# Two attentions of a transformer kernel: a zero-padded tile that stays allocated, and a second buffer for copies out of PSUM

## The chip, the cores and the metric

The kernel runs on one core of a Trainium2 chip. The metric is the device time of one execution in microseconds, the median of several runs. Five engines work side by side, each on its own queue of instructions in a fixed order: PE (matmuls; its weight loads are shown as PEld), DVE, ACT, POOL, and SP, which issues the DMAs. An instruction at the head of a queue that has to wait holds up everything behind it on that engine.

## The reference, cut to what matters

Two layers over 1024 tokens of width 1024. Layer 0 mixes with a hybrid attention (8 dilated heads and 4 pairs of differential heads), layer 1 with a latent attention of 16 heads; after each comes a feed-forward block with a short convolution. Both attentions are causal softmax attentions over blocks of 128 queries:

```python
def one_block(args):
    i, qi = args
    qpos = i * Q_BLOCK + jnp.arange(Q_BLOCK)
    causal = kpos[None, :] <= qpos[:, None]
    s = jnp.einsum('bqhd,bkhd->bhqk', qi, k).astype(jnp.float32) * scale
    p = jax.nn.softmax(jnp.where(causal, s, -jnp.inf), axis=-1)
    return jnp.einsum('bhqk,bkhd->bqhd', p.astype(v.dtype), v)
```

The kernel carries each fp32 operand as a high and a low part and adds several products of the parts.

## The kernel before, in words

Work runs through these stages in turn: the first attention with its projections (to about 540 us), the first feed-forward block, the second attention (about 1318 to 1664 us), the second feed-forward block.

In both attentions a head is worked off in two groups, g = 0 (query blocks 0 to 3, in the order 1, 0, 3, 2) and g = 1 (blocks 4 to 7). For each block `scores` has PE form the scores in a `wide` PSUM tile (L250, two such tiles), DVE take scale, mask and row maximum into `prob` (L259), and ACT the exponential (L262). `turn_parts` then writes the normalised probabilities as two fp16 parts into `hl`: the high part by ACT (L286) and the low part by DVE (L287), except for block 3 (`LP`), where ACT scales (L283) and POOL makes both parts (L121 and L110). SP transposes `hl` by DMA into `pTa`, `pTb` or `pT` (L290, L293), and `weigh` has PE multiply these with the values V (L327).

Blocks 0 and 1 share one tile, `hl01` (shown in the trace as `hl`): four quarter tiles for key blocks and query blocks, of which the quarter "key block 1, query block 0" must be zero. Before, each group g = 0 allocates this tile anew from one buffer, and POOL writes its zeros (L277) before the parts go in. The new tile's first write has to wait until the DMA transposition (L293) of the group before has read the old one. There are 28 such groups: 12 in the first attention, 16 in the second.

In the second attention, `prep(p)` makes queries, keys and values of the next pair of heads in the background, in a budget of PE time beside the current groups. `nope` multiplies into a PSUM tile `bank_t` (three of them serve all such work), ACT copies it to an SBUF tile `stage` (L1380), and POOL makes from it the high parts (L1384) and the low parts (L110) for two heads: four instructions for each copy. `values` does the same with `vs` (L1398), which shares the tag and so the buffer of `stage`: two POOL instructions for each copy (L121, L110). With one buffer, a copy waits until POOL is done with the one before. The first pair (p = 0) splits straight out of PSUM and uses no such copy.

The order of instructions on each engine is written when the program is built: the Tile layer plays the instructions against modelled durations (`schedule_with_timeline_sim=True`) and gives each engine the most urgent instruction whose inputs and buffers are ready in that model. Urgency is program order, with a bonus of 30 places for the maximum and the exponential. On the chip the order is fixed; when an instruction takes longer than the model had it, what stands behind it waits.

Of the kernel before, what the change touches and what calls it, by code (L numbers as in the profile page):

```python
# [11 lines left out]
F32 = mybir.dt.float32  # L12
F32R = mybir.dt.float32r
I32 = mybir.dt.int32
F16 = mybir.dt.float16
# [6 lines left out]
P = 128  # L22
# [24 lines left out]
def model_kernel(ctx: ExitStack, tc: tile.TileContext, a: dict, out: bass.AP, dbg: dict):  # L47
    nc = tc.nc
# [21 lines left out]
    def bank_p():  # L70
        if ps_lat[0]:
            return ps[0].tile([P, 512], F32, name="bank_p", tag="bank_p", bufs=1)
        return bank_t()
# [38 lines left out]
    def dma(out_, in_):  # L112
        out_, in_ = (v.bitcast(F32) if v.dtype == F32R else v for v in (out_, in_))
        nc.sync.dma_start(out=out_, in_=in_)

    def split(hi, lo, x, lo_eng=None):
        nc.scalar.copy(out=hi, in_=x)  # L117
        sub(lo_eng or nc.vector, lo, x, hi)

    def pool_split(hi, lo, x):  # L120
        nc.gpsimd.tensor_scalar(out=hi, in0=x, scalar1=1.0, scalar2=1.0, op0=ALU.mult, op1=ALU.mult)  # L121
        sub(nc.gpsimd, lo, x, hi)

    def mm3(out_, sh, sl, mh, ml, start, stop):
        nc.tensor.matmul(out_, sh, mh, start=start, stop=False)  # L125
        nc.tensor.matmul(out_, sh, ml, start=False, stop=False)  # L126
        nc.tensor.matmul(out_, sl, mh, start=False, stop=stop)  # L127
# [137 lines left out]
    def turn_parts(pt, l, top, i, pool, pts):  # L265

        r = pool.tile([P, 1], F32, name="rl", tag="rl", bufs=6)
        nc.vector.reciprocal(out=r, in_=l)
        nc.vector.tensor_scalar(out=r, in0=r, scalar1=top, scalar2=1.0, op0=ALU.mult, op1=ALU.mult)
        pair = MERGE and i < 2  # L270
        if not pair:
            hl = pool.tile([P, i + 1, 2, P], F16, name="hl", tag="hl", bufs=PH[1])
            hi, lo = hl[:, :, 0, :], hl[:, :, 1, :]
        else:
            if len(pts) == 2:
                hl = pool.tile([P, 2, 2, 2, P], F16, name="hl01", tag="hl01", bufs=1)
                nc.gpsimd.memset(hl[:, 1, :, 0, :], 0.0)  # L277
                pts.append(hl)
            hl = pts[2]
            hi, lo = hl[:, :i + 1, 0, i, :], hl[:, :i + 1, 1, i, :]  # L280
        v = pt.rearrange("p (k c) -> p k c", c=P)
        if i in LP:
            nc.scalar.activation(out=v, in_=v, func=AF.Copy, scale=r)  # L283
            pool_split(hi, lo, v)
        else:
            nc.scalar.activation(out=hi, in_=v, func=AF.Copy, scale=r)  # L286
            nc.vector.scalar_tensor_tensor(out=lo, in0=v, scalar=r, in1=hi, op0=ALU.mult, op1=ALU.subtract)  # L287
        if not pair:
            j = (i - 2) % 4 if MERGE and i < 4 else i % 4
            nc.sync.dma_start_transpose(out=pts[-1 if i > 3 else 1][:, :2 * (i + 1), j * P:(j + 1) * P],  # L290
                                        in_=hl.rearrange("p k s c -> p (k s c)"))
        elif len(pts) == 4:
            nc.sync.dma_start_transpose(out=pts[0].rearrange("p n (i q) -> p (n i) q", i=2),  # L293
                                        in_=hl.rearrange("p k s i c -> p (k s i c)"))
        else:
            pts.append(None)

    def new_pts(pool, g):
        if g:
            return [pool.tile([P, 16, 512], F16, name="pT", tag="pT", bufs=1)]  # L300
        return [pool.tile([P, 4, 256], F16, name="pTa", tag="pTa", bufs=1),
                pool.tile([P, 8, 256], F16, name="pTb", tag="pTb", bufs=1)]
# [489 lines left out]
    def open_pool(name, side="left"):  # L792
        return tc.alloc_tile_pool(name=name, bufs=1, side=side, reuse_waits="tile")
# [331 lines left out]
    pool = open_pool("hyb_n")  # L1125
# [20 lines left out]
        nc.sync.dma_start(out=d, in_=t)  # L1146
    pool.release()
    pool = open_pool("hyb_at", "right")
    made = []

    def tail_hyb():
# [168 lines left out]
    def new_QK(pool):  # L1320
        i = len(QK)
        QK.append([{n: pool.tile([P, 2, S], F32R, name=f"{n}{par}{i}") for n in "qk"}
                   for par in range(2)])
        for n in "qk":
            nc.gpsimd.memset(QK[i][1][n][0:32].bitcast(F32), 0.0)
# [13 lines left out]
    def prep(p):  # L1339

        qd = p // 2
        T = QK[p % 2]
        ws = slice((p % 2) * P, (p % 2 + 1) * P)
        if p % 2 == 0:
            quads[qd] = [kp.tile([P, 2, S], F32R, name="rhl", tag="rhl", bufs=1),
                         kp.tile([P, NB, 2, 2, P], F16, name="V4", tag="V4", bufs=2)]
        rhl, V = quads[qd]

        def turn(hf):
            pt = bank_p()  # L1350
            for j in range(4):
                nc.tensor.transpose(pt[:, j * P:(j + 1) * P],
                                    qr[:, hf * 4 + j, qd * P:(qd + 1) * P], ident)
            ts = slice(hf * 512, (hf + 1) * 512)
            split(rhl[:, 0, ts], rhl[:, 1, ts], pt)
            yield 428

        def q_rope(ts):
            for par in range(2):
                hd = (p % 2) * 2 + par  # L1360
                src = slice(hd * 32, hd * 32 + 32)
                dma(T[par]["q"][ROWS[par][1], :, ts], rhl[src, :, ts])

        def nope(hf):
            ts = slice(hf * 512, (hf + 1) * 512)
            for n, chunks in (("q", (0, 1)), ("k", (2,))):
                wh, wl = w[n]
                o = bank_p()
                for ci, c in enumerate(chunks):
                    mm3(o, wh[:, ci, ws], wl[:, ci, ws], cTh[:, c, ts], cTl[:, c, ts],  # L1370
                        ci == 0, ci == len(chunks) - 1)
                    if ci < len(chunks) - 1:
                        yield 640
                if p == 0:
                    for par in range(2):
                        rows = ROWS[par][0]
                        split(T[par][n][rows, 0, ts], T[par][n][rows, 1, ts], o[rows])
                else:
                    st = ap.tile([P, 512], F32, name="stage", tag="stage", bufs=1)
                    nc.scalar.copy(out=st, in_=o)  # L1380
                    for par in range(2):
                        rows = ROWS[par][0]
                        t = T[par][n][rows]
                        nc.gpsimd.tensor_scalar(out=t[:, 0, ts], in0=st[rows],  # L1384
                                                scalar1=1.0, scalar2=1.0, op0=ALU.mult, op1=ALU.mult)
                        sub(nc.gpsimd, t[:, 1, ts], st[rows], t[:, 0, ts])
                yield 640

        def values(hf):
            for b in range(4 * hf, 4 * hf + 4):  # L1390
                bs = slice(b * P, (b + 1) * P)
                o = bank_p()
                mm3(o[:, :256], cTh[:, 2, bs], cTl[:, 2, bs], w["v"][0][:, 0], w["v"][1][:, 0],
                    True, True)
                ov = o[:, :256].rearrange("p (h d) -> p h d", d=P)
                if p:
                    vs = ap.tile([P, 2, P], F32, name="vs", tag="stage", bufs=1)
                    nc.scalar.copy(out=vs, in_=ov)  # L1398
                    pool_split(V[:, b, :, 0], V[:, b, :, 1], vs)
                else:  # L1400
                    split(V[:, b, :, 0], V[:, b, :, 1], ov)
                yield 320

        halves = [slice(0, 512), slice(512, S)]
        if p == 0:
            w = qw[0]
            for hf in range(2):
                yield from turn(hf)
                q_rope(halves[hf])
                k_rope(0, halves[hf])  # L1410
                yield from nope(hf)
                yield from values(hf)
            return
        if p % 2 == 0:
            for hf in range(2):
                yield from turn(hf)
            next(quad_gen[-1])
        w = qw[qd]
        q_rope(slice(0, S))
        for hf in range(2):  # L1420
            yield from nope(hf)
        if p % 2 == 0:
            for hf in range(2):
                yield from values(hf)
        elif p < 7:
            quad_gen.append(quad_weights(qd + 1, bank_p))
            next(quad_gen[-1])
# [45 lines left out]
    PH[:] = BUF_MLA  # L1473
    psum("ps_mla")
    ap = open_pool("mla_at")
    new_QK(ap)
    k_rope(1, slice(0, S))
    run_slot([[groups[0][0](), groups[0][1], 0.0], [bgs[0], P_COST / 2 + V_COST / 2, 0.0]], None)
# [144 lines left out]
```

## Time and profile before

| | us |
|---|---|
| median of 3 runs | 2417.92 (2417.5 to 2418.85) |
| the profiled execution's own time | 2414.22 |
| its span from first to last instruction | 2412.4 |
| mean granted TensorE clock in the span | 0.979 of full speed |

Times in the rows are microseconds from the first instruction of the profiled execution. An engine's busy time in a stretch does not add up with that of the others, since they run side by side.

### The profile page before, as it was taken

What the parts mean: (1) busy time and instruction counts of PE and PEld (TensorE: products, weight loads), DVE (VectorE), ACT (ScalarE), POOL (GpSimd) and SP (SyncE); (2) the same over time, 40 slices, a digit from 0 to 9 for tenths busy, and PEclk for the clock granted to TensorE, in tenths of its full rate; (3) what the DMA queues carried; (4) which work ended last, traced back from release to release, by engine and by line L of the source; (5) the groups of instructions that cost most, each with busy time, mean ns of one, the idle gap of its engine ahead of it and who ended that gap; (6) DMA issues with size and microseconds to landing.
All of it is one profiled execution on the core that took longest, in us unless ns stands there. A gap on an engine that the chain in (4) does not pass through costs nothing. (4 is left out here: it accounts for less than half of the span.)

```text
span 2412.4 us, 32458 instructions
## 1 busy us (share of the span) xinstructions
PE 2222.4 (92%) x11216; PEld 1254.7 (52%) x11216; DVE 1941.0 (80%) x3265; ACT 1551.8 (64%) x2633; POOL 1115.2 (46%) x1157
## 2 busy tenths in 40 slices
PE   7999999898999999999999888889899999999998
PEld 5555566675444444343457666667644444434443
DVE  6777788848788888888786886875778888888887
ACT  6787776636766565666445887764576757575743
POOL 3233333116446464645126777741554656464621
PEclk9999999999999999999999998999999999999999
DMA  4566642651211111111031898797221112121101
GB/s 147 112 133 133 139 94 63 172 176 36 79 53 62 44 62 44 62 53 59 13 128 34 161 170 170 151 278 201 74 70 58 66 37 70 43 70 44 62 27 70
DMA packets 322358, 224.28 MB, mean 93 GB/s; under 512 B 279120, under 2 KB 282192, under 8 KB 321744
## 3 DMA queue, kind: packets, MB, share of 16 engines
q1 hardware_dynamic: 322192, 222.20, 35.5%
q8 instruction: 88, 1.44, 0.2%
q14 instruction: 78, 0.64, 0.1%
HBM read 123.59 MB, written 25.43 MB: 62 GB/s over the span
## 5 line engine op out<-in xcount | busy, mean ns | idle before, releaser
L572 PEld LDWEIGHTS <-up_h 128*128 128x128 f16 x2464 | 239.1, 98 | 319.2 <-issue 46.2
L262 ACT ACTIVATE prob<-prob,m 128x512 f32<-128x512 f32 (+7 forms) x256 | 197.5, 772 | 76.6 <-DVE m L259 61.1
L287 DVE SCALAR_TENSOR_TENSOR hl<-prob,rl,hl 128x896 f16<-128x896 f32 (+6 forms) x196 | 185.8, 957 | 41.3 <-ACT hl L286 40.0
L572 PEld LDWEIGHTS <-up_l 128*128 128x128 f16 x1232 | 120.8, 98 | 150.0 <-issue 7.9
L651 DVE SCALAR_TENSOR_TENSOR up_l<-up_raw,wsc,up_h 128x1024 f16<-128x1024 f32 x84 | 137.4, 1637 | 61.7 <-ACT up_h L650 61.7
L286 ACT ACTIVATE hl<-prob,rl 128x896 f16<-128x896 f32 (+6 forms) x196 | 149.0, 775 | 47.4 <-DVE prob L1031 15.1
L125 PE MATMUL bank_t<-hw_h,hTh 128*128 128x384 f16 x512 | 170.0, 334 | 7.4 <-ACT hw_h L650 4.4
L126 PE MATMUL bank_t<-hw_l,hTh 128*128 128x384 f16 x512 | 169.9, 333 | 0.6 <-DVE hw_l L651 0.5
L127 PE MATMUL bank_t<-hw_h,hTl 128*128 128x384 f16 x512 | 169.9, 332 | 0.0
L259 DVE CUSTOM_DVE_ANT_0 prob<-wide,maskc 128x256 f32<-128x256 f32 (+3 forms) x192 | 142.7, 750 | 23.5 <-PE wide L250 20.0
L731 PEld LDWEIGHTS <-qah 128*128 128x128 f16 x896 | 86.3, 98 | 124.0 <-issue 20.5
L250 PE MATMUL wide<-k,q 96*128 96x512 f32 (+7 forms) x576 | 131.7, 366 | 17.6 <-DVE m L259 17.2
L327 PEld LDWEIGHTS <-V 128*128 128x128 f16 x1064 | 97.0, 99 | 90.5 <-issue 33.7
L737 DVE SCALAR_TENSOR_TENSOR x<-bank_a,gun,x 128x512 f32<-128x512 f32 x168 | 124.4, 743 | 18.5 <-PE bank_a L731 14.9
L737 DVE SCALAR_TENSOR_TENSOR x<-bank_b,gun,x 128x512 f32<-128x512 f32 x152 | 112.7, 743 | 24.2 <-PE bank_b L731 24.2
L488 ACT ACTIVATE up_s<-up_raw 128x1024 f32<-128x1024 f32 x88 | 92.9, 1056 | 61.0 <-DVE up_l L651 33.4
L327 PE MATMUL bank_o<-pT,V 128*128 128x512 f16 (+3 forms) x608 | 120.3, 351 | 12.7 <-DMA pT<-hl 8.5
L110 POOL TENSOR_TENSOR up_l<-up_raw,up_h 128x512 f16<-128x512 f32 (+1 forms) x48 | 69.6, 1450 | 129.0 <-ACT up_h L117 75.0
L250 PEld LDWEIGHTS wide<-k,q 128*128 128x128 f32 (+1 forms) x576 | 98.7, 198 | 37.0 <-DVE m L259 22.9
L578 ACT COPY u<-prod 128x512 f32<-128x512 f32 x176 | 96.9, 572 | 29.2 <-PE prod L572 27.5
L650 ACT ACTIVATE dn_h<-dn_raw,dsc 128x1024 f16<-128x1024 f32 (+1 forms) x60 | 60.5, 1030 | 74.9 <-PE bank_b L731 52.3
L650 ACT ACTIVATE up_h<-up_raw,wsc 128x1024 f16<-128x1024 f32 x84 | 95.1, 1141 | 19.4 <-DVE wsc L459 14.6
(441 smaller groups left out, 7077.9 us busy)
## 6 DMA issues: line engine op xcount, KB each, us to landing
up_raw<-in_w_up_dram SPq DMA_DIRECT2D x88, 512.0 KB, 3.8
dn_raw<-in_ffn_w_down_dram SPq DMA_DIRECT2D x44, 512.0 KB, 3.2
hw_raw<-in_w_hyb_dram SPq DMA_DIRECT2D x32, 384.0 KB, 3.7
OTa<-ohl SPq DMA_DIRECT2D x16, 512.0 KB, 2.7
oa<-OTa SPq DMA_DIRECT2D x16, 512.0 KB, 6.3
OTb<-ohl SPq DMA_DIRECT2D x16, 512.0 KB, 3.4
x<-in_x_dram SPq DMA_DIRECT2D x8, 512.0 KB, 8.3
wo_raw<-in_hyb_w_out_dram SPq DMA_DIRECT2D x16, 256.0 KB, 3.3
```

Of the source, the lines that this page charges most:

```text
L125: nc.tensor.matmul(out_, sh, mh, start=start, stop=False)
L126: nc.tensor.matmul(out_, sh, ml, start=False, stop=False)
L127: nc.tensor.matmul(out_, sl, mh, start=False, stop=stop)
L250: nc.tensor.matmul(sp[:, h * 512:h * 512 + w], q[:, qs], k[:, c:c + w], start=n == 0, stop=n == len(passes) - 1)
L259: nc.vector.tensor_tensor_reduce(out=pv, in0=sv, in1=mv, scale=-scale, scalar=3e38, op0=ALU.add, op1=ALU.min, accum_out=m)
L262: nc.scalar.activation(out=pv, in_=pv, func=AF.Exp, bias=m, scale=-1.0, accum_out=l)
L286: nc.scalar.activation(out=hi, in_=v, func=AF.Copy, scale=r)
L287: nc.vector.scalar_tensor_tensor(out=lo, in0=v, scalar=r, in1=hi, op0=ALU.mult, op1=ALU.subtract)
L327: nc.tensor.matmul(o[:, c:c + w], s, v, start=kb == 0 and n == 0, stop=kb == last and n == len(todo) - 1)
L572: nc.tensor.matmul(o, w[side][p][:, k], blocks[block][q][:, k], start=first and k == n == 0, stop=k == 3 and n == 2, skip_group_check=not ...
L650: nc.scalar.activation(out=h, in_=x, func=AF.Copy, scale=s)
L737: nc.vector.scalar_tensor_tensor(out=x_, in0=m, scalar=un, in1=x_, op0=ALU.mult, op1=ALU.add)
```

## The change

`hl01` becomes one tile for each attention, allocated when the attention's pool is opened; its zero quarter is written there once, and all groups g = 0 of that attention write their parts into the same tile. The zero quarter is never written by the parts. `stage` and `vs` get two buffers in place of one. The pool of the second attention grows by 2 KB in each partition for it.

```diff
         else:
+            hl = first_hl[0]
             if len(pts) == 2:
-                hl = pool.tile([P, 2, 2, 2, P], F16, name="hl01", tag="hl01", bufs=1)
-                nc.gpsimd.memset(hl[:, 1, :, 0, :], 0.0)
                 pts.append(hl)
-            hl = pts[2]
             hi, lo = hl[:, :i + 1, 0, i, :], hl[:, :i + 1, 1, i, :]
...
+    first_hl = [None]
+
+    def new_first(pool):
+
+        first_hl[0] = pool.tile([P, 2, 2, 2, P], F16, name="hl01")
+        nc.gpsimd.memset(first_hl[0][:, 1, :, 0, :], 0.0)
...
     pool = open_pool("hyb_at", "right")
+    new_first(pool)
...
-                    st = ap.tile([P, 512], F32, name="stage", tag="stage", bufs=1)
+                    st = ap.tile([P, 512], F32, name="stage", tag="stage", bufs=2)
                     nc.scalar.copy(out=st, in_=o)
...
-                    vs = ap.tile([P, 2, P], F32, name="vs", tag="stage", bufs=1)
+                    vs = ap.tile([P, 2, P], F32, name="vs", tag="stage", bufs=2)
                     nc.scalar.copy(out=vs, in_=ov)
...
     ap = open_pool("mla_at")
+    new_first(ap)
     new_QK(ap)
```

## Rows read from the trace of the kernel before

**Rows 1.** The page's first part: busy time, share of the span and instructions of each engine.

```profile
PE 2222.4 (92%) x11216; PEld 1254.7 (52%) x11216; DVE 1941.0 (80%) x3265; ACT 1551.8 (64%) x2633; POOL 1115.2 (46%) x1157
```

**Rows 2.** Stretches (first attention, second attention, its end): us, engines' busy (instructions), PEclk, DMA share, GB/s.

```profile
60.00:500.00 440.00, 412.06 (x2458) 271.86 (x2455) 353.70 (x866) 318.35 (x623) 123.23 (x157) 0.97 0.55 122
1318.00:1600.00 282.00, 237.84 (x1304) 175.76 (x1302) 227.05 (x595) 219.43 (x452) 211.51 (x225) 0.95 0.86 174
1600.00:1664.00 64.00, 62.40 (x326) 46.75 (x327) 44.28 (x102) 39.66 (x70) 8.61 (x9) 0.97 0.95 229
```

**Rows 3.** What PE waited for from 1318 to 1600: us in total, times, longest us.

```profile
PE wide L250 <- DVE m L259: 17.2, 16, 3.7
...
PE bank_t L125 <- ACT vs L1398: 4.4, 5, 2.3
PE bank_t L1229 <- ACT stage L1380: 2.8, 2, 2.0
...
PE bank_t L125 <- ACT stage L1380: 2.2, 2, 1.3
```

**Rows 4.** What ACT waited for from 1318 to 1600, same columns.

```profile
ACT stage L1380 <- POOL q L110: 8.9, 7, 2.0
...
ACT vs L1398 <- POOL V L110: 5.6, 4, 1.9
ACT stage L1380 <- POOL V L110: 2.4, 2, 1.3
...
ACT stage L1380 <- POOL k L110: 1.0, 2, 0.7
```

**Rows 5.** Timeline of PE: start, us, instruction, [idle before it, what ended that].

```profile
1383.64 0.39 PE L125 MATMUL bank_t<-w4vh,cTh 128*128 128x256 f32 x1 [0.92 <-ACT stage L1380]
...
1421.64 0.19 PE L1229 MATMUL bank_t<-kvg,wsq 128*128 128x2 bf16 x2 [2.01 <-ACT stage L1380]
...
1483.98 0.50 PE L125 MATMUL bank_t<-cTh,w4qh 128*128 128x512 f32 x1 [2.34 <-ACT vs L1398]
...
1504.08 0.19 PE L1229 MATMUL bank_t<-kvg,wsq 128*128 128x2 bf16 x2 [0.75 <-ACT stage L1380]
```

**Rows 6.** Timeline of ACT, same columns.

```profile
1383.00 0.59 ACT L1380 COPY stage<-bank_t 128x512 f32<-128x512 f32 x1 [1.74 <-POOL q L110]
...
1421.01 0.59 ACT L1380 COPY stage<-bank_t 128x512 f32<-128x512 f32 x1 [1.96 <-POOL q L110]
...
1503.44 0.59 ACT L1380 COPY stage<-bank_t 128x512 f32<-128x512 f32 x1 [1.56 <-POOL q L110]
```

**Rows 7.** Stretches of 4 us in the second attention, columns as in rows 2.

```profile
1424.00:1428.00 4.00, 4.00 (x16) 3.07 (x15) 3.06 (x9) 3.52 (x8) 3.75 (x5) 0.65 0.36 67
...
1484.00:1488.00 4.00, 4.00 (x13) 3.28 (x14) 2.05 (x12) 3.49 (x9) 2.67 (x5) 0.61 1.14 237
...
1504.00:1508.00 4.00, 3.43 (x14) 2.99 (x14) 3.54 (x16) 4.00 (x14) 3.65 (x4) 0.67 0.93 171
```

**Rows 8.** Line 277, all instructions; then what ended its engine's idle time (us, times).

```profile
L277 POOL MEMSET hl<- x28: 302/312/317, 54.9 to 1631.5; 128x256 f16 x28
...
  DMA pTa<-hl: 42.6, 15
```

**Rows 9.** Timeline of POOL in the first attention.

```profile
407.35 0.31 POOL L277 MEMSET hl<- 128x256 f16 x1 [5.86 <-DMA pTa<-hl]
407.74 0.62 POOL L121 TENSOR_SCALAR hl<-prob 128x512 f16<-128x512 f32 x1
```

**Rows 10.** A stretch of 6 us in the first attention, columns as in rows 2.

```profile
402.00:408.00 6.00, 6.00 (x37) 3.85 (x36) 5.18 (x16) 2.60 (x6) 0.57 (x2) 1.00 0.23 44
```

**Rows 11.** POOL's groups from 1318 to 1600: busy us, mean ns, idle before and its releasers.

```profile
L110 POOL TENSOR_TENSOR q<-stage,q 64x512 fp32r<-64x512 f32 x28 | 40.2, 1434 | 1.9
...
L1384 POOL TENSOR_SCALAR q<-stage 64x512 fp32r<-64x512 f32 x28 | 21.4, 766 | 5.3 <-ACT stage L1380 4.2
```

**Rows 12.** Line 121 from 1318 to 1600: duration ns min/median/max, first and last start.

```profile
L121 POOL TENSOR_SCALAR hl<-prob x14: 615/621/977, 1331.4 to 1592.4; 128x512 f16<-128x512 f32 x14
```

## Prediction, made before the changed kernel had run

> **What bounds the kernel now.** I read the page's busy times first, for the engine that has least room; then the stretches of the two attentions, since the change touches nothing else; then, in the stretch where there is something to gain, what PE and ACT waited for; last single places in the timelines.
>
> Over the whole span PE is busy 92% of the time, and POOL, which both edits relieve, 46% [rows 1]. An average over stages decides nothing here. In the first attention PE is busy 412.06 of 440 us (94%) and POOL 123.23 (28%). In the second, from 1318 to 1600, PE is busy only 237.84 of 282 us (84%), while DVE, ACT and POOL have 227.05, 219.43 and 211.51 (81%, 78%, 75%): no engine is full, and the stretch is set by who waits for whom. From 1600 to 1664, when the background work on the next heads has run out and the output projection fills in, PE is at 97% [rows 2]. So the 44 us for which PE stands idle between 1318 and 1600 are the place to look; what is saved there moves all that follows, the next block too, by as much.
>
> The reader is to see two things in the waits of that stretch. PE waited nine times, 9.4 us together (4.4 + 2.8 + 2.2), for ACT to empty a `bank_t` tile into `stage` or `vs` [rows 3]. And ACT waited fifteen times, 17.9 us together, for POOL to be done with the one buffer of these copies (8.9 + 5.6 + 2.4 + 1.0) [rows 4]. PE's largest wait, 17.2 us for DVE to empty a `wide` tile [rows 3], has another origin and stays.
>
> **The change part by part.** *Zeros written once.* Of 28 memsets of 312 ns two remain: 26 x 0.31 = 8.1 us less POOL work, and none of POOL's 42.6 us of waiting at these memsets for the transposition that still reads the old tile [rows 8]. What it is worth depends on what stands behind them on POOL. In the first attention the worst place is at 407.35: the memset waited 5.86 us and the split of block 3, which PE's value product needs later, starts right behind it [rows 9]. But PE was busy 6.00 of the 6 us from 402 to 408 [rows 10], with the projection of the next heads, which is that place's cover. I take 0 for the first attention. The bounds: a gain of 5.9 us if this longest wait lay bare, and a loss of nothing but an order made worse (below). In the second attention the wait stands ahead of splits out of `stage` and `vs`, so it lengthens the waits of rows 4 and is counted with them. The two memsets that remain move to the opening of the pools: 0.31 us each ahead of the attention's first POOL work, 0.6 us if nothing hid it. The writes of the parts keep the wait that the tile's reuse always meant: ACT's and DVE's writes for blocks 1 and 0 must still follow the transposition of the group before. Two buffers are not given here, so no transposition starts earlier.
>
> *Two buffers for the copies.* No instruction is added or removed. A copy now waits for POOL to finish not the copy before it but the one before that. One `stage` copy costs POOL two conversions and two subtractions, 2 x (0.766 + 1.434) = 4.4 us by the rows for `q`; `k` is alike [rows 11]. The longest of ACT's waits is 2.0 us [rows 4], less than that, so with a second buffer all 17.9 us of these waits should go, except where two copies follow each other within one POOL turn. The price: none in instructions; in SBUF a tile that fits beside the others.
>
> What of it reaches PE? Three of the nine PE waits come straight after a copy that itself had waited for POOL: PE at 1383.64, 1421.64 and 1504.08 (0.92 + 2.01 + 0.75 = 3.7 us) behind ACT at 1383.00, 1421.01 and 1503.44 (1.74, 1.96 and 1.56 us idle) [rows 5, 6]. These I count in full. The other six (9.4 - 3.7 = 5.7 us, the largest 2.34 us at 1483.98) come behind a copy that ACT issued late without standing idle. Its place in ACT's order was planned with one buffer in mind, and a new plan can put it earlier; between 0 and 5.7 I take half, 2.9. Sum: 6.6 us.
>
> [...]
>
> [...]
>
> The rest of ACT's waiting (17.9 less the 5.3 us of rows 6, 12.6 us) delays exponentials and with them DVE. PE kept busy meanwhile, so I count 0, with 12.6 as the far bound.
>
> [...]
>
> Sum: 6.6 + 3.5 = 10.1 us. PE's gaps from other causes are 44 - 9.4 = 35 us, 12% of the stretch; a PE that comes earlier runs into some of them, and longer. I take off a fifth, by choice: 8 us. From the profiled execution: 2414.2 - 8 = 2406.2. Its own time lies 3.7 us under the median of the runs (2414.22 against 2417.92), so the median to expect is 2409.9.
>
> **The rivals.** A change under 0.2% (4.8 us) is about what a measurement of this kernel can't tell from none.
>
> *The gaps only move.* The queues are in a fixed order made from modelled durations, and a removed memset or a free buffer changes the order of all that follows. If each copy that comes sooner only lets PE reach the next `wide` tile that DVE hasn't emptied (17.2 of PE's 44 us already [rows 3]), what stays is little; I put it at 2 us: 2415.9. For it speaks that DVE and ACT are nearly as busy as PE. Against it, that PE reaches 97% as soon as it has work without these copies [rows 2]. This takes in the case that the edits don't act: the memset's waits hide wholly, and the copies find POOL the slower in any case.
>
> [...]
>
> *POOL's queue turns against the softmax (slower than before).* With one buffer POOL never had more than one copy's splits before it. With two, 4.4 us of further splits can stand ahead of block 3's split, of which there are 14 in the stretch [rows 12]; it, and the transposition that takes its result, come late, and PE's value product stands in a fixed place. It decides from the point at which PE loses more than (8 + 4.8) / 14 = 0.9 us for each: at 1.3 us it is 18 us against the 8 gained, 2427.9. For it: POOL's durations vary (615 to 977 ns for the first instruction of this split [rows 12]), and splits are planned as soon as a buffer is free. Against: product and split are a whole group apart, and the splits behind the second buffer have to be done in either case.
>
> [...]
>
> **How the numbers follow.** Forecast 0.46 (own range 2404 to 2414), gaps only move 0.24, more comes back 0.16, POOL's queue 0.14. Of the forecast 0.03 lies above 2413.1, and of the moved gaps 0.02 above 2422.8. Faster by over 0.2%: 0.43 + 0.16 = 0.59. Within: 0.03 + 0.22 = 0.25. Slower: 0.02 + 0.14 = 0.16. The range reaches down to 2397, past the 20 us, and up to 2425, where the POOL case has begun; outside lie about 0.05 below and 0.1 above.
>
> **What would show it.** Two memsets of 128x256 are left, and POOL no longer waits on `pTa`. ACT's waits at L1380 and L1398 for POOL fall from 17.9 us to under 4, PE's for these copies from 9.4 to under 4. The stretch from 1318 to 1600 shortens by about 8 us and the low clock near 1424 and 1504 is gone, while both feed-forward blocks and the first attention keep their lengths to 2 us. The prediction is wrong if ACT's waits go and PE's gaps grow elsewhere by as much (`wide` on `m`, `bank_o` on `pT`), if block 3's split starts later behind its scaling, or if the first attention, where I expect nothing, moves by more than 3 us.

## The result, and the profile after

The change made the kernel slower: 2430.72 us median (2426.82 to 2432.53, 4 runs) against 2417.71 for the kernel before beside it, a ratio of 1.0051 with a 95% interval of 1.004 to 1.0063. The forecast was 2409.9, in a range of 2397 to 2425. Sign and size were wrong.

The page's busy times of the changed kernel, to be set beside [rows 1]:

```profile
PE 2228.3 (92%) x11216; PEld 1257.8 (52%) x11216; DVE 1942.1 (80%) x3265; ACT 1549.6 (64%) x2633; POOL 1104.5 (46%) x1131
```

POOL has 26 instructions less, as the step on the zeros had it, and 10.7 us less (8.1 were worked out); it no longer waits for `pTa` anywhere. The three stretches of [rows 2], after:

```profile
60.00:500.00 440.00, 412.95 (x2466) 273.71 (x2464) 356.04 (x864) 316.90 (x623) 120.30 (x146) 0.97 0.54 122
1318.00:1600.00 282.00, 237.12 (x1278) 175.13 (x1279) 222.72 (x570) 211.13 (x435) 206.86 (x210) 0.92 0.82 169
1600.00:1664.00 64.00, 55.56 (x286) 40.29 (x285) 41.61 (x106) 38.39 (x74) 8.51 (x8) 0.97 0.94 217
```

The first attention is where it was. In the second PE is busy as long as before and gets less done (1278 matmuls against 1304) at a lower granted clock (0.92 against 0.95), and from 1600 to 1664 it is busy 55.56 us against 62.40. A stretch at fixed times hides what that costs, so here is the whole second attention between two marks, from the start of the last DMA that writes `x` out to `xs` to the start of ACT's last copy of outputs out of PSUM (`of`). First the kernel before, then the one after; columns as in [rows 2]:

```profile
1269.20:1674.00 404.80, 356.71 (x1927) 269.45 (x1926) 306.54 (x758) 286.37 (x587) 252.69 (x307) 0.96 0.77 163
```

```profile
1270.50:1687.50 417.00, 360.98 (x1928) 272.15 (x1927) 309.34 (x759) 285.86 (x587) 248.40 (x292) 0.94 0.74 158
```

The same matmuls take 12.2 us longer. PE is idle 417.00 - 360.98 = 56.0 us against 48.1 (+7.9), and busy 4.3 us longer at the lower clock (0.94 against 0.96). What stands ahead of the first mark takes 1.3 us more than before, and what follows the second 1.2 (to the end of the span, 739.6 against 738.4): the loss is the second attention's.

What ACT and PE waited for from 1318 to 1600, beside [rows 3, 4]; us, times, longest us:

```profile
ACT prob L262 <- DVE m L259: 23.6, 16, 5.2
...
ACT stage L1386 <- POOL q L110: 2.5, 2, 1.3
ACT vs L1404 <- POOL q L110: 2.1, 1, 2.1
ACT stage L1386 <- POOL V L110: 1.8, 3, 0.7
ACT stage L1386 <- POOL k L110: 1.8, 1, 1.8
...
ACT vs L1404 <- POOL V L110: 0.7, 1, 0.7
```

```profile
PE bank_o L332 <- DMA pT<-hl: 7.4, 6, 2.1
PE bank_o L332 <- DMA pTb<-hl: 7.1, 2, 4.4
PE wide L250 <- DVE m L259: 5.6, 8, 1.7
PE bank_o L332 <- ACT of L1456: 4.9, 3, 3.7
PE bank_t L125 <- ACT vs L1404: 4.5, 4, 1.9
PE wide L250 <- DVE rl L269: 4.5, 3, 2.5
...
PE wide L250 <- POOL k L1390: 2.6, 1, 2.6
...
PE bank_t L125 <- ACT stage L1386: 0.9, 2, 0.4
```

The second buffer did a part of what was asked of it: ACT's waits for POOL fell from 17.9 to 8.9 us, PE's for the copies from 9.4 to 5.4. PE's wait for `m` fell too, from 17.2 to 5.6 (from 17.2 to 9.6 between the two marks). In their place stand waits in front of the products with V (`bank_o`: 7.1 us for the transposition into `pTb`, before under 0.4, and 4.9 for the copy `of`, before 2.3) and in front of `wide` (4.5 for `rl`, 2.6 for `k`; before under 0.4 each). And ACT now stands idle longer for DVE's row maximum `m`; between the two marks, before and after:

```profile
ACT prob L262 <- DVE m L259: 20.1, 23, 2.4
```

```profile
ACT prob L262 <- DVE m L259: 39.1, 27, 5.2
```

PE's largest single wait, with PE, DVE, POOL and SP of the changed kernel in turn (SP's line holds two transpositions):

```profile
1482.24 2.35 PE L250 MATMUL wide<-k,q 128*128 128x512 f32 x12
1484.43 0.60 PE L1358 MATMUL bank_t<-ident,qr 128*128 128x128 f32 x4
1486.12 0.27 PE L332 MATMUL bank_o<-pTa,V 128*128 128x256 f16 x1 [1.10 <-ACT of L1456]
1490.76 0.37 PE L332 MATMUL bank_o<-pTb,V 128*128 128x256 f16 x1 [4.36 <-DMA pTb<-hl]
1490.92 0.42 PE L332 MATMUL bank_o<-pTa,V 128*128 128x256 f16 x1
```

```profile
1481.67 1.39 DVE L339 TENSOR_SCALAR wsc<-cst 128x2 int32<-128x2 int32 x1
...
1483.30 1.01 DVE L352 TENSOR_SCALAR cst<-cst 128x2 f32<-128x2 f32 x1
...
1484.35 0.17 DVE L339 TENSOR_SCALAR cst<-cst 128x2 int32<-128x2 int32 x1
...
1485.00 5.20 DVE L285 SCALAR_TENSOR_TENSOR hl<-prob,rl,hl 128x384 f16<-128x384 f32 x3
1490.13 1.08 DVE L259 CUSTOM_DVE_ANT_0 prob<-wide,maskc 128x896 f32<-128x896 f32 x1
```

```profile
1481.88 1.16 POOL L110 TENSOR_TENSOR hl<-prob,hl 128x512 f16<-128x512 f32 x1
1483.00 1.28 POOL L110 TENSOR_TENSOR q<-stage,q 64x512 fp32r<-64x512 f32 x1
```

```profile
1486.12 2.56 SPq L288 DMA_TRANSPOSE pTb<-hl  x2
```

The product with `pTb` needs the transpositions of blocks 2 and 3. DVE's low part for block 2 (the 128x384 one) starts at 1485.00, behind small operations of the background that scale the next weights. POOL holds these up (more on it in the last section): the one at 1481.67 took 1.39 us and ended with POOL's split of block 3, the one at 1483.30 took 1.01 and ended with POOL's next subtraction, and one like the first, at 1484.35, took 0.17. SP has block 2's transposition first: it issues it at 1486.12, when the low part is done, and it lands 2.8 us later. Block 3's parts were ready on POOL by 1483.0, but its transposition stands behind in SP's order: it is issued at 1487.43 and lands 3.3 us later, at 1490.7, and this is what PE waits for. PE's product stands next in PE's order and there are no scores between. ACT idles 5.2 us at the same place for the maximum that stands behind those low parts. PE's granted clock, 1.00 from 1480 to 1488, is 0.56 and 0.59 in the two stretches of 4 us from 1488 on: behind the wait the clock is low as well.

Is it this order, then, or one of the edits? A new buffer rule changes the planned order of everything behind it, so each experiment below was also laid beside the others as an order: the sequence of instructions that the build writes for each engine, leaving out the memsets of zeros.

### The profile page after: what moved, and what is told of

Same layout as the page of the kernel before. It is cut to its first block, busy times and chain, and to the rows that moved or that the text cites. A ratio compares the mean times of both kernels' runs of the same rounds, so it can differ in the third digit from the quotient of the medians.

```text
span 2427.1 us, 32393 instructions
## 1 busy us (share of the span) xinstructions
PE 2228.3 (92%) x11216; PEld 1257.8 (52%) x11216; DVE 1942.1 (80%) x3265; ACT 1549.6 (64%) x2633; POOL 1104.5 (46%) x1131
## 5 line engine op out<-in xcount | busy, mean ns | idle before, releaser
L262 ACT ACTIVATE prob<-prob,m 128x512 f32<-128x512 f32 (+7 forms) x256 | 197.4, 771 | 106.1 <-DVE m L259 83.4
L285 DVE SCALAR_TENSOR_TENSOR hl<-prob,rl,hl 128x128 f16<-128x128 f32 (+6 forms) x196 | 187.6, 962 | 43.5 <-ACT hl L284 41.6
L656 DVE SCALAR_TENSOR_TENSOR up_l<-up_raw,wsc,up_h 128x1024 f16<-128x1024 f32 x84 | 132.5, 1582 | 54.8 <-ACT up_h L655 53.1
L284 ACT ACTIVATE hl<-prob,rl 128x128 f16<-128x128 f32 (+6 forms) x196 | 149.3, 774 | 36.3 <-DVE prob L1036 13.8
L259 DVE CUSTOM_DVE_ANT_0 prob<-wide,maskc 128x256 f32<-128x256 f32 (+3 forms) x192 | 143.0, 751 | 26.6 <-PE wide L250 22.9
L250 PE MATMUL wide<-k,q 96*128 96x512 f32 (+7 forms) x576 | 130.7, 368 | 17.4 <-DVE m L259 9.6
L250 PEld LDWEIGHTS wide<-k,q 128*128 128x128 f32 (+1 forms) x576 | 99.2, 200 | 35.4 <-DVE m L259 16.5
L516 POOL TENSOR_TENSOR up_raw<-up_raw,up_s 128x512 f32<-128x512 f32 x44 | 74.6, 1694 | 90.8 <-DVE pw L456 45.7
```

What stands on the lines that cost most here:

```text
L250: nc.tensor.matmul(sp[:, h * 512:h * 512 + w], q[:, qs], k[:, c:c + w], start=n == 0, stop=n == len(passes) - 1)
L262: nc.scalar.activation(out=pv, in_=pv, func=AF.Exp, bias=m, scale=-1.0, accum_out=l)
L656: nc.vector.scalar_tensor_tensor(out=l, in0=x, scalar=s, in1=h, op0=ALU.mult, op1=ALU.subtract)
```

## Experiments: each edit by itself, and the place of the copies

Three explanations stood at first: the copies are planned ahead of the softmax; the buffers themselves cost; any change replans the order, and the direction is chance.

**Tile alone** and **buffers alone**:

```diff
-                    st = ap.tile([P, 512], F32, name="stage", tag="stage", bufs=2)
+                    st = ap.tile([P, 512], F32, name="stage", tag="stage", bufs=1)
```

(and `vs` likewise) on the changed kernel gives tile_only; the same two lines of the change alone, on the kernel before, give buffers_only.

> The zero-padded tile stays allocated as in the changed kernel, the copies keep one buffer. Theory 1 (the second attention's background work is planned ahead of the softmax, and that costs): in ACT's planned order an average copy stands after 56.4 exponentials of the second attention, against 60.1 before and 49.5 in the changed kernel, so about a third of the loss of 13 us, 2420 to 2424. Theory 2 (the buffers themselves cost, by what POOL and ACT do at once): no loss, 2414 to 2418. Theory 3 (any change throws the planned order anew, the direction is chance): anything from 2408 to 2430, with no bond to the place of the copies.

> Two buffers for the copies, the tile with its 28 memsets as before. Theory 1: an average copy stands after 50.4 exponentials, nearly as in the changed kernel, so nearly the whole loss, 2427 to 2432. Theory 2: the whole loss, 2428 to 2432. Theory 3: anything from 2408 to 2430.

Measured: tile_only 2412.81 us, ratio 0.9997 (0.9987 to 1.0007); buffers_only 2409.96, ratio 0.9985 (0.9969 to 1.0001). Neither edit is slow (and buffers_only's gain isn't clear of none). The first two explanations had both forecast the loss for buffers_only. The loss belongs to the two edits together.

**Copies held back** behind the newest exponential (kept in `last_exp`), in the changed kernel (copies_held) and in the one before (before_held), for `stage` as shown and for `vs` likewise; `issue_after` sets a place in the order and no wait:

```diff
-                    nc.scalar.copy(out=st, in_=o)
+                    with tc.issue_after(last_exp[0]):
+                        nc.scalar.copy(out=st, in_=o)
```

> The changed kernel in full, but each copy of the background work is queued on ACT behind the exponential that the program wrote last before it (order of issue alone, nothing waits for a result). An average copy then stands after 59.0 exponentials, as before the change (60.1), while two buffers and the lasting tile stay. Theory 1: the loss goes, and with the waits for POOL gone too the kernel is at 2405 to 2418. Theory 2: the loss stays, 2426 to 2432. Theory 3: anything from 2408 to 2430.

> The kernel before, with the same order of issue for its copies (behind the exponential written last): an average copy stands after 62.9 exponentials. It shows what the holding does by itself. Theory 1: within 5 us of the kernel before, since the copies stand later than the best place by little; slower if they are now so late that the next heads wait. Theory 2: as before, 2414 to 2420. Theory 3: anything from 2408 to 2430.

Measured: copies_held 2423.06, ratio 1.0038 (1.0025 to 1.0051); before_held 2417.11, ratio 1.0012 (1.0001 to 1.0023). Putting the copies back took about a quarter of the loss away (1.0051 to 1.0038, with intervals that overlap), and buffers_only has its copies as early as the changed kernel (an average one behind 50.4 exponentials against 49.5) and isn't slow. That the copies run ahead of the softmax is not the cause.

## Experiments: which attention, and is it the zeros or the order?

All from here on have two buffers.

**Zeros each time** in the lasting tile; **lasting in one attention only**, with a tile and zeros in each group in the other; **one column of zeros** (in each of the two parts) each time:

```diff
             if len(pts) == 2:
+                nc.gpsimd.memset(hl[:, 1, :, 0, :], 0.0)     # zeros_each
+                nc.gpsimd.memset(hl[:, 1, :, 0, 0:1], 0.0)   # zeros_tiny
                 pts.append(hl)
...
-    new_first(ap)                                            # lasting_first_only
+    first_hl[0] = None
...
-    new_first(pool)                                          # lasting_second_only
```

> Two buffers and the lasting tile, but its zeros are written again in each of the 28 groups, as before. The built order of all five engines is then that of buffers_only, instruction for instruction. Theory A (the loss is the order of the second attention that follows from leaving out the zeros, together with the second buffer): 2407 to 2413 us, as buffers_only (2410.0). Theory D (that the tile lasts costs by itself, by its place in memory or its longer life): 2420 or more, as the full change.

> Two buffers, lasting tile in the first attention only; the second attention has a tile and zeros in each group. Order: the first attention is that of the full change, the second that of buffers_only. Theory A: 2407 to 2413 us, the second attention's stretch as in buffers_only. Theory B (the first attention's new order, or a state that it leaves, costs the time): 2422 to 2432. Theory C (any new order is a throw of the dice of half a per cent): anything from 2405 to 2430, with the stretch differing from that of buffers_only although the order there is the same.

> Two buffers, lasting tile in the second attention only; the first attention has the order of the kernel before, the second that of the full change but for a few places near its end. Theory A: 2422 to 2432 us, with PE again waiting for the copies of the outputs and for the parts' transposes between 1400 and 1620. Theory B: 2407 to 2413.

> Two buffers, lasting tile, and in each of the 28 groups one column of zeros written again (1 of 256 elements a partition): the groups are tied to the memset as before, but its work is nearly nothing. The built order of the second attention is close to that of the full change (POOL differs in 21 of 1128 places, PE in 339 of 19561). Theory A: 2420 to 2430 us, near the full change. Theory E (it is the tie, the wait for the transposes that the memset puts into POOL's queue, that held POOL back usefully): 2407 to 2413.

| | us | ratio | 95% interval |
|---|---|---|---|
| zeros_each | 2411.85 | 0.9987 | 0.9975 to 0.9999 |
| lasting_first_only | 2411.93 | 0.9991 | 0.9978 to 1.0005 |
| lasting_second_only | 2433.57 | 1.0069 | 1.0046 to 1.0093 |
| zeros_tiny | 2425.81 | 1.004 | 1.0026 to 1.0053 |

The four came out as theory A has it (lasting_second_only 1.6 us above its range). The lasting tile costs nothing by itself (zeros_each has buffers_only's order throughout and its time), the first attention's new order is worth nothing, and the loss sits in the second attention, with two buffers and no zeros there. But A still has two readings: the missing memsets let POOL run where it shouldn't, or the order planned without them is bad. The next kernels part these.

**Order against work.** A counter of the groups writes the zeros in some of the second attention's 16 groups g = 0 only (turn counts them from 0), or a part of their columns in all 28:

```diff
+                if first_hl[1] and turn >= 4:                # zeros_late12; turn < 4: zeros_first4
+                    nc.gpsimd.memset(hl[:, 1, :, 0, :], 0.0)
...
+                nc.gpsimd.memset(hl[:, 1, :, 0, 0:32], 0.0)  # zeros_2x32; 0:44: zeros_2x44
```

> The full change, with zeros written again in the last 12 of the second attention's 16 first-block groups (not in its first 4, nor in the first attention). The built order of the five engines is that of the full change, place for place, with 12 memsets (0.31 us each) let into POOL's. Theory A (the loss is the order of the second attention): 2422 to 2433 us, as the full change. Theory F (the loss is the missing memset itself, its work or its wait, which braked POOL): back most of the way, 2410 to 2418.

> The counterpart: zeros written again in the first 4 of the 16 groups only. The built order is then close to that of the fast kernels (178 of 19561 places of PE differ from lasting_first_only, against 1104 from the full change), though 12 of 16 memsets are gone. Theory A: 2407 to 2415 us. Theory F: 2420 to 2428.

> The full change, with 2 x 32 of the 2 x 128 columns of zeros written again in every group. The built order of the second attention is near that of the full change (269 PE places differ; 1710 from buffers_only). Theory A: 2420 to 2431 us. Theory C (any order is a throw of the dice): no relation to which of the two it is near.

> The same with 2 x 44 columns: 24 elements more a partition in each memset, some tens of ns by the two durations seen (0.107 us for 2 elements, 0.312 us for 256), but the built order flips to near that of buffers_only (384 PE places differ; 1676 from the full change). Theory A: 2407 to 2415 us, some 14 us below zeros_2x32. Theories E and F (the memset's work or wait): the same as zeros_2x32 within 3 us.

| | us | ratio | 95% interval |
|---|---|---|---|
| zeros_late12 | 2426.03 | 1.0046 | 1.0028 to 1.0064 |
| zeros_first4 | 2409.58 | 0.9982 | 0.9973 to 0.9992 |
| zeros_2x32 | 2426.27 | 1.0045 | 1.003 to 1.006 |
| zeros_2x44 | 2417.04 | 1.001 | 1.0001 to 1.0019 |

Twelve memsets put back without moving the order give nothing back; four that move it give everything back. Between 32 and 44 columns, 9.2 us go, with next to no work (zeros_2x44 was expected at 2415 at most). The order decides.

## Experiments: what in the order

In the built order of PE one can count how many score matmuls (L250) have been issued before a group's first product that reads `pTb` (before its first product, where g = 1): the lead that the softmax has been given. The mean over the 32 groups is 323.9 to 324.3 in the two-buffer kernels that beat the one before, 323.3 in zeros_2x44, and 319.0 to 320.2 in those that lose 0.4% and more. One kernel doesn't fit from the start: copies_held has 322.4 and loses 0.38%. Four more orders test whether time follows it (theory G):

```diff
+                nc.gpsimd.memset(hl[:, 1, :, 0, 0:112], 0.0) # zeros_2x112; 0:120: zeros_2x120
...
+                if first_hl[1] and turn < 2:                 # zeros_first2; turn >= 2: zeros_from3rd
+                    nc.gpsimd.memset(hl[:, 1, :, 0, :], 0.0)
```

> 2 x 112 of the 2 x 128 columns of zeros written in every group. Work and waits of the memsets as good as in zeros_each (2411.9 us), but the built order has a count of 320.3 score matmuls ahead of a group's outputs, near zeros_tiny (320.2). Theory G (the count decides): 2421 to 2430 us. Theory C (chance): no relation to the count. Theory F (the memsets' work and waits decide): 2408 to 2415.

> 2 x 120 columns: count 319.8, near zeros_2x32 (320.0). Theory G: 2421 to 2430 us. Theory F: 2408 to 2415. Theory C: anything.

> The zeros written again in the first 2 of the 16 groups only. Count 322.1: the order stands ahead as in the fast kernels for the first 21 groups and as in the slow ones from group 24 on. Theory G: 2414 to 2421 us, the second attention like zeros_first4 up to about 270 us after its start and late only from there.

> The zeros written again in all but the first 2 groups. Count 324.2, as in the fast kernels. Theory G: 2407 to 2414 us. Theory C: anything.

| | count | us | ratio | 95% interval |
|---|---|---|---|---|
| zeros_2x112 | 320.3 | 2415.64 | 1.0005 | 0.9996 to 1.0015 |
| zeros_2x120 | 319.8 | 2424.98 | 1.0043 | 1.0027 to 1.006 |
| zeros_first2 | 322.1 | 2418.48 | 1.0017 | 1.0004 to 1.0029 |
| zeros_from3rd | 324.2 | 2410.53 | 0.9979 | 0.9969 to 0.999 |

Three of four are where G puts them; zeros_2x112 is 5 us below its range. The count goes with the time among most kernels with two buffers, then, but is not the whole of it, and the kernel before does well with 320.6. A sign that parts the kernels better is ACT's wait for the row maximum (`prob` L262 for `m` L259 in the full change) between the two marks, in one profiled execution of each. It is 20.1 to 29.7 us in the kernel before and in nine others with ratios up to 1.0012 (the one-buffer kernels among them), and 35.6 to 42.8 us in the nine with 1.0017 and more, copies_held (35.7) among them; zeros_2x112 alone (36.8 us at 1.0005) is on the wrong side. It is a symptom of the slower orders; that it is their cause was not tested. What zeros_first2 adds is a place: from the 8th to the 25th of the 32 groups it copies its outputs out of PSUM within 2 us of zeros_first4 (the 25th 314.4 us after the first mark against 315.3). From there its order is that of the slower kernels, and the last group comes at 406.9 against 398.7.

**Two memsets, twice.** Last, a pair with the same work to the last instruction:

```diff
+                if first_hl[1] and turn in (1, 2):           # two_in_2nd_3rd; (0, 3): two_in_1st_4th
+                    nc.gpsimd.memset(hl[:, 1, :, 0, :], 0.0)
```

> The full change, with the zeros written again in the 2nd and 3rd of the second attention's 16 groups only: two memsets of 0.31 us more than the full change has. Its built order is that of zeros_first4 (count 323.9 score matmuls ahead of a group's outputs). The order decides: 2407 to 2413 us, ratio 0.997 to 0.9995, ahead of the kernel before. The work or the waits decide: as the next kernel within 2 us.

> The same two memsets, in the 1st and the 4th group instead. Its built order has the count of the full change (319.1). The order decides: 2423 to 2432 us, 12 to 20 above the kernel that it is paired with. The work or the waits decide: the same time within 2 us.

Measured: two_in_2nd_3rd 2406.57 us, ratio 0.9971 (0.9961 to 0.9981); two_in_1st_4th 2426.0, ratio 1.0052 (1.0037 to 1.0067). Two memsets of 0.31 us, in other groups, are worth 19.4 us. The first has the order of zeros_first4, the second that of the full change, place for place on all five engines. Between the two marks, first two_in_2nd_3rd, then two_in_1st_4th:

```profile
1269.50:1665.30 395.80, 353.93 (x1928) 269.36 (x1927) 309.03 (x759) 286.42 (x588) 249.21 (x294) 0.97 0.80 167
```

```profile
1268.60:1687.50 418.90, 362.36 (x1928) 272.09 (x1927) 309.17 (x759) 285.58 (x587) 248.66 (x294) 0.94 0.74 158
```

PE's idle time is 41.9 and 56.5 us, its busy time 353.9 and 362.4. Of the 23.1 us between them 14.6 are waits and 8.4 longer busy time for the same 1928 matmuls, at a granted clock of 0.94 against 0.97. Where they arise is read from the copies of outputs (11th, 16th and last of 32), first of two_in_2nd_3rd, then of the full change, whose first mark is 1.0 us later:

```profile
1442.62 0.58 ACT L1461 COPY of<-bank_o 64x512 f32<-64x512 f32 x1
...
1499.46 0.58 ACT L1461 COPY of<-bank_o 64x512 f32<-64x512 f32 x1
...
1665.30 0.58 ACT L1461 COPY of<-bank_o 64x512 f32<-64x512 f32 x1 [9.39 <-PE bank_o L337]
```

```profile
1451.22 0.58 ACT L1456 COPY of<-bank_o 64x512 f32<-64x512 f32 x1
...
1512.65 0.58 ACT L1456 COPY of<-bank_o 64x512 f32<-64x512 f32 x1 [1.27 <-PE bank_o L332]
...
1687.51 0.58 ACT L1456 COPY of<-bank_o 64x512 f32<-64x512 f32 x1 [10.40 <-PE bank_o L332]
```

So the full change is 7.6 us behind by 1451, 12.2 by 1513, and 21.2 at the end: the loss is gathered at many places. At the one place of the 4.36 us wait, PE of two_in_2nd_3rd, and its stretches from 1480 on:

```profile
1480.29 0.27 PE L337 MATMUL bank_o<-pTa,V 128*128 128x256 f16 x1 [2.89 <-ACT of L1461]
1480.94 2.29 PE L250 MATMUL wide<-k,q 96*128 96x256 f32 x6 [0.38 <-DVE m L259]
1483.03 0.44 PE L337 MATMUL bank_o<-pTb,V 128*128 128x256 f16 x1
1483.26 0.42 PE L337 MATMUL bank_o<-pTa,V 128*128 128x256 f16 x1
```

```profile
1480.00:1484.00 4.00, 3.33 (x12) 2.20 (x12) 3.88 (x14) 2.62 (x8) 3.93 (x3) 0.60 1.10 201
1484.00:1488.00 4.00, 4.00 (x22) 3.57 (x21) 2.35 (x7) 3.89 (x8) 3.75 (x4) 0.55 1.05 197
```

Here six score matmuls of later blocks stand between the group's first product and the one that needs `pTb`; the full change has none there. When PE comes to the product, the last transposition has landed, at 1482.5. But the faster order isn't free of waits at this place: PE stood 2.89 us for the copy `of` and 0.38 for `m`, and the granted clock was 0.60 and 0.55 in the two stretches behind them (1.00 from 1488 on), about as low as in the full change. The scores in between save some 2 us of idle time here (3.3 against 1.10 + 4.36), a part of the 14.6, and nothing of the clock. Nor is it a general pattern: of the 16 groups g = 0, 12 have no scores at that point in either kernel. Over the whole second attention PE's idle time grows from two_in_2nd_3rd to two_in_1st_4th in front of `wide` (14.5 to 18.6 us), `pT` (6.6 to 10.9), `pTb` (4.3 to 7.2) and `bank_t` (7.3 to 10.2).

## Why the prediction was wrong

**The zeros.** The removed work was as said, and the first attention, for which I took 0, added at most the 1.3 us at the mark; tile_only's 0.9997, and lasting_first_only's 0.9991 beside buffers_only's 0.9985, agree. The later zeros of the second attention count for nothing either: twelve of them put back left the time at 1.0046.

**The second buffer.** The waits that it was to shorten did become shorter, by less than said for ACT: from 1318 to 1600 ACT's for POOL are 3.5 us in copies_held and 7 to 12 in all other kernels with two buffers, not under 4 (8.9 in the full change; before, a wait of 0.3 us for `k` comes on top of the 17.9), and PE's for the copies 0.6 to 5.7 (5.4). But the time doesn't follow them: copies_held, with ACT's smallest (3.5) and 2.2 of PE's, and zeros_2x32, with 1.2 of PE's, lose 0.38% and 0.45%. Alone the buffers came to 0.9985, 3.6 us faster at the median. two_in_2nd_3rd, the full change in a better order, is 7.3 us faster at the median (2406.57 against 2413.84), and between the marks 9.0 us shorter than before (395.8 against 404.8): 6.2 of idle time and 2.8 of busy time (granted clock 0.97 against 0.96), where the sum had 6.6 and 3.5 less a fifth, 8. That this comes so near is luck, since its order is another one too and orders differ by more than that. No run shows the sum's 3.5 us for the clock: what the runs showed is those 2.8 us less of busy time in this order, and 4.3 us more in the full change, whose clock was 0.94. The nine gaps of [rows 3] were 9.4 us together; in the full change 4.0 us of them went and the time rose.

**The step that failed** is the one from the sum to the forecast: "I take off a fifth, by choice". It lets the old order stand and has PE come a little earlier in it; a new order is put at nothing there. In fact each of the two edits gave all five engines a new order in the second attention, and both together another. Thirteen different orders with two buffers ran here, the same work but for some zeros; they lie between 0.9971 and 1.0069, some 24 us apart (19.4 in the closest comparison, the last pair), two to three times the gain that I worked out. Kernels with one and the same order agree to about 0.001 (0.9985 and 0.9987; 0.9982 and 0.9971; 1.0046, 1.0051 and 1.0052), so this is no scatter of the measurement. A forecast that follows old waits into a new order has that width, and mine had a chance of 0.16 for slower.

**The rivals.** "The gaps only move" named the replanned order and PE's idle time from 1318 to 1600 is indeed the same (44.9 against 44.2 us), but I priced it at 2 us gained and it went on to the loss. "POOL's queue turns against the softmax" forecast 2427.9, near the time measured, but for a reason that the trace doesn't show: the delay of block 3's split on POOL behind its scaling on ACT, summed over the 16 of them, is 21.2 us after and 21.4 before, and at the place of the 4.36 us wait block 3's parts had been ready for 4 us when SP issued their transposition. What POOL did there was to hold up DVE's small operations. That more comes back, 20 us faster at the low end of the range, was an estimate of mine that no run showed: the fastest, two_in_2nd_3rd, gained 7.3 us.

**What would show it.** The granted clock near 1424 and 1504 rose (1.00 and 0.81 in the same stretches, against 0.65 and 0.67 in [rows 7]) and was low in other places (0.56 from 1488 to 1492). The sign named for a wrong prediction, ACT's waits gone and PE's gaps grown elsewhere (`bank_o`), is what came.

**What stays open.** The order is shown to be the cause, by kernels whose work is the same. That the softmax's shorter lead before the products is what the slower orders have wrong fits eleven of thirteen counts (not copies_held and zeros_2x112), and is not proved: no run changed one place and left the rest of the order as it was. Why two memsets flip the plan lies in the planner's modelled durations and is left open.

## What to carry to other kernels

Where a planner writes the order, an edit has two prices, its own and that of the new order, and the second can be the larger, with either sign. Before a small edit is believed or dropped, run it in a few orders that do the same work (a trifle of work moved or added is enough) and compare kernels of equal order; here the full change with two redundant memsets in the right groups beats both the kernel before (0.9971) and the full change. In an order itself, look at what stands between a product and the transposition it needs, and in the DMA queue ahead of that transposition: at the one place followed here, scores of later blocks covered a part of the wait, and in both orders PE's granted clock was low behind a wait (0.56 and 0.59, 0.60 and 0.55), on top of the idle time. And a wait that shrinks as planned proves no gain: compare the whole stage between two marks of the program.

## What the runs showed of the hardware that was not expected

DVE's low part (one `scalar_tensor_tensor` with both its large inputs in SBUF) of 128x384 took 1.06 us in the full change at 1485, and the two behind it 2.02 and 2.28 (means from 1318 to 1600: 1.11 for 768 columns, 1.56 for 1024), while POOL was in splits of `stage`, whose subtractions took 1.56 and 1.98 us against a mean of 1.43 in [rows 11]. In two_in_2nd_3rd, where POOL beside it had only a 128x2 operation, the same low part took 0.60:

```profile
1472.29 0.60 DVE L289 SCALAR_TENSOR_TENSOR hl<-prob,rl,hl 128x384 f16<-128x384 f32 x1
```

```profile
L285 DVE SCALAR_TENSOR_TENSOR hl<-prob,rl,hl 128x1024 f16<-128x1024 f32 x1 | 2.3, 2281 | 0.0
L285 DVE SCALAR_TENSOR_TENSOR hl<-prob,rl,hl 128x768 f16<-128x768 f32 x1 | 2.0, 2016 | 0.0
...
L285 DVE SCALAR_TENSOR_TENSOR hl<-prob,rl,hl 128x384 f16<-128x384 f32 x1 | 1.1, 1058 | 0.0
```

(The second fence is DVE's groups in the full change from 1484.9 to 1490.2: busy us, mean ns, idle before.) Where no POOL instruction ran beside them in the second attention of the full change, low parts of 384, 768 and 1024 columns took 0.60 to 0.62, 1.01 to 1.02 and 1.28 us; the three at 1485 took 1.7 to 2 times as long, and POOL's subtractions beside them up to 1.4 times their mean. Running at the same time doesn't by itself slow DVE: in the full change a low part of 768 columns that began just ahead of such a subtraction took the 1.02 us that it takes alone, and POOL's took 2.04:

```profile
1404.58 1.02 DVE L285 SCALAR_TENSOR_TENSOR hl<-prob,rl,hl 128x768 f16<-128x768 f32 x1 [0.80 <-ACT hl L284]
```

```profile
1404.70 2.04 POOL L110 TENSOR_TENSOR q<-stage,q 64x512 fp32r<-64x512 f32 x1
```

DVE's smallest operations pay most for their size. In the second attention of the full change 12 of its TENSOR_SCALARs of 128x2 elements go from SBUF to SBUF (lines 339, 352 and 354). Ten of them took 0.46 to 1.39 us and ended 0.03 us after a POOL instruction that ran beside them; the other two took 0.16 and 0.17. Two of the ten are the 1.39 and 1.01 us ahead of PE's wait of 4.36 us.
